# A hybrid S5 and gated-DeltaNet layer on one core: when the adaLN gate, shift and scale vectors are computed, and which queue loads their weights

## The chip, the cores and the metric

The kernel runs on one core of a Trainium2 chip. The metric is the device time of one execution in microseconds; lower is better. Engines are named as the profile names them: PE (matmul) with its weight loads PEld, DVE (vector), ACT (scalar), POOL (GpSimd) and SP (which here only issues DMAs). The program gives each engine one fixed order of instructions.

## The reference, cut to what matters

One layer, 512 tokens, width 2048, float32. `mod` gives six vectors of 2048: shift, scale and gate of the mixer, shift, scale and gate of the feed-forward part.

```
mod = (silu(c) @ w_ada + b_ada)                  # w_ada is 2048 x 12288: 100 MB
sh_m, sc_m, g_m, sh_f, sc_f, g_f = split(mod, 6)
h = layer_norm(x) * (1 + sc_m) + sh_m
p = h @ w_in
ys = s5(p) @ w_up_ssm;  yg = gated_deltanet(p) @ w_up_gdn        # "the mixers"
m = sigmoid(gate_ssm) * ys + sigmoid(gate_gdn) * yg              # "merge"
x = layer_norm(alpha * x + g_m * (m @ w_out), ln1_g, ln1_b)      # "output projection"
h = layer_norm(x) * (1 + sc_f) + sh_f
x = layer_norm(alpha * x + g_f * swiglu(h), ln2_g, ln2_b)        # feed-forward, hidden 5632
```

So g_m is first needed behind the output projection, sh_f and sc_f when the second norm is applied, and g_f when the first feed-forward sums are added.

## The kernel before

**Products.** Every large product is made of three float32r matmuls: weights and activations are each split into a high part (rounded on ACT: `whi`, `at`/`bt`) and a low part (the difference, on DVE: `wlo`). `Weights` walks one list of weight chunks of 512 KB: a load on SP into one of NB = 3 `raw` buffers, a cast to `whi` on ACT, a subtraction to `wlo` on DVE, then the matmuls into `pm` or `px_fo`. A `raw` buffer is free for the next load when its `wlo` has been computed.

**Stages, in order of PE's program.** Start (x, adaLN shift and scale of the mixer). The mixers: `gemm1` products of the eight DeltaNet heads, with the S5 scan and the DeltaNet chunk solve between them. At `switch()` the mixers' buffers are given up and two pools `bp` and `q2` (`P2`) take their place; then the remaining gate products, the GLU, and the merge. The output projection (`w_mix`, 64 chunks, 12 matmuls of 512 columns each) runs in two halves of 256 tokens. Then the feed-forward part: its first eight hidden tiles are computed in two token halves with matmuls of 256 columns, because the second norm of the second token half (`ln_half(1)`) is still under way; everything later is done on 512 tokens. `ln_half(hf)` normalizes (DVE, ACT, POOL), applies the second norm into `ld`, transposes on PE into `px_tr`, applies scale and shift `mod_f` on ACT (`f`) and splits the result into `h2`.

**What sets the order.** The kernel is written by a small planner (`Order`): side work is a set of generators ("lines"); each yield gives the tile that the line waits for, or a pause in microseconds of the planner's own clock, and after each matmul of the main line `tick()` writes the steps that are due by that clock. The result is one fixed order for each engine.

**The adaLN vectors.** Each vector is made in four lines of 512 columns. `ada_line` loads 16 chunks of 256 KB (128 rows x 512 columns) into `w1` (called `w` in the profile; four buffers, for a while also two `gg` buffers) and adds `chunk * ccol` into `aacc`: in the kernel before, eleven of the sixteen on DVE, five on ACT with POOL adding them into `aacc2`, and one DVE addition at the end; the loads are issued on POOL. `ada_row_line` then adds the bias, sums over partitions on PE (`px_ada<-aacc,half`) and writes 512 values to DRAM (`drow[2]`, in the profile `dgm`, for g_m; `drow[5]`, `dgf`, for g_f), from which they are later read back as rows (`grow`). `ada_cols_line` sums on PE with `one` and writes a piece of `mod_f`. The line `ada_rest` makes g_m (four row lines), then shift and scale (eight column lines), then g_f (four row lines), and is started in `switch()`. Three flags tell others how far it is: `k.ada_m` (waited for at the output projection's `grow`), `k.ada_f` (waited for in `ln_half` ahead of the transposes), `k.ada_done` (waited for ahead of the first feed-forward sums).

Of the kernel before, what the change touches and what calls it, by code (L numbers as in the profile page):

```python
# [11 lines left out]
F32 = mybir.dt.float32  # L12
# [949 lines left out]
def kernel(ctx, tc, x, c, w_ada, b_ada, w_in, lam_re, lam_im, log_dt, b_re, b_im, c_re, c_im,  # L962
# [5 lines left out]
    k = Ctx()  # L968
    o = k.o = Order()
# [152 lines left out]

    def ada_line(p, col0):

        acc = p.tile([128, 512], F32, name="aacc", tag="aacc", bufs=1)
        acc2 = P2[1].tile([128, 512], F32, name="aacc2", tag="aacc2", bufs=1) if P2 else None
        raws = []
        depth = 6 if k.ada_deep else 4

        def load():  # L1130
            k0 = 128 * len(raws)
            n = k.ada_n = k.ada_n + 1
            if not k.ada_deep or n % 6 < 4:
                raw = p.tile([128, 512], F32, name="w1", tag="w1", bufs=4)
            else:
                raw = P2[1].tile([128, 512], F32, name="gg", tag="gg", bufs=2)
            pool.dma_start(out=raw, in_=w_ada[0, k0:k0 + 128, col0:col0 + 512])
            raws.append(raw)
        for kt in range(16):
            while len(raws) < min(16, kt + depth):  # L1140
                load()
            yield raws[kt]
            while not P2 and o.free["v"] > o.clock + 0.2:
                yield 0.7
# [15 lines left out]
    def ada_cols_line(p, j, q, dst, plus):  # L1160

        acc = yield from ada_line(p, 2048 * j + 512 * q)
        yield acc
        ps = k.psum("ada")
        for i in range(4):
            pe.matmul(ps[:, i:i + 1], lhsT=acc[:, 128 * i:128 * i + 128], rhs=one, start=True, stop=True)
        v.scalar_tensor_tensor(out=dst, in0=ps[:, 0:4], scalar=plus, in1=bcol[:, 16 * j + 4 * q:16 * j + 4 * q + 4], op0=A, op1=A)

    def ada_row_line(p, j, q):

        acc = yield from ada_line(p, 2048 * j + 512 * q)
        for i in range(4):
# [6 lines left out]
        act.copy(acc[0:1, :], ps[0:1, :])  # L1179
        yield  # L1180
        ld.dma_start(out=drow[j][0:1, 512 * q:512 * q + 512], in_=acc[0:1, :])
# [164 lines left out]
    P2 = []  # L1346
    k.ada_m = k.ada_f = k.ada_done = k.ada_deep = False
    k.ada_n = 0

    def ada_rest():  # L1350
        for q in range(4):
            yield from ada_row_line(adp, 2, q)
        k.ada_m = True
        for q in range(4):
# [3 lines left out]
        for q in range(4):  # L1358
            yield from ada_row_line(adp, 5, q)
        k.ada_done = True  # L1360


# [428 lines left out]
```

## Time and profile before

| | us |
|---|---|
| runs, median of 3 (lowest to highest) | 3185.92 (3182.63 to 3190.62) |
| profiled execution, its own time | 3192.52 |
| its span, first to last instruction | 3190.7 |
| PE busy in the span | 3039.6 (95%) |
| DVE, ACT, POOL busy | 1649.5, 976.4, 879.7 |
| mean granted TensorE clock | 0.976 |

Places in the span, read from the times of the matmuls: the mixers run to about 1082, when the first `w_ada` load of `ada_rest` is issued; remaining gates, GLU and merge to 1431; output projection 1431 to 1656; then the transposes of the first token half; the first feed-forward tiles on 256 tokens each from 1682 and 1790 to 1890; the rest on 512 tokens. A PE that is busy is not a PE at full rate: matmuls overlap, so the number of matmuls in a stretch says more than the busy time.

### The profile page before, as it was taken

How to read it: one execution, taken by the hardware profiler on the slowest of the kernel's cores; microseconds unless marked ns; L12 is line 12 of the kernel's file. 1: busy time of each engine (PE TensorE's matmuls, PEld its weight loads, DVE VectorE, ACT ScalarE, POOL GpSimd, SP SyncE). 2: the span in 40 equal slices, each digit the busy share in tenths (PEclk: the TensorE clock that was granted, in tenths of full speed). 3: DMA queues.
4: the chain of work that ended last, by engine and by line, in shares of the span. 5: the costliest groups of instructions: out<-in, count | busy, mean ns of one | idle time of the engine just before them, and what ended most of it. 6: DMA issues, size and time to landing. Idle time of an engine off the chain costs nothing.

```text
span 3190.7 us, 40575 instructions
## 1 busy us (share of the span) xinstructions
PE 3039.6 (95%) x15953; PEld 2507.5 (79%) x15953; DVE 1649.5 (52%) x2407; ACT 976.4 (31%) x1386; POOL 879.7 (28%) x997
## 2 busy tenths in 40 slices
PE   5899999999999999998878899999999999999997
PEld 3588788888788888886758798888888888888885
DVE  6536664566545377767778653333333333333338
ACT  3233333333333244334345531221222222222121
POOL 4824434434352143333344203002001100200202
PEclk8899999999999999999989999999999999999999
DMA  9644233333333488778878463333333333333333
GB/s 339 217 126 109 72 82 92 93 88 81 84 98 86 152 283 267 235 246 290 272 232 242 137 177 108 94 99 111 94 99 108 97 99 104 101 99 97 108 106 119
DMA packets 505344, 458.17 MB, mean 144 GB/s; under 512 B 56144, under 2 KB 403632, under 8 KB 505152
## 3 DMA queue, kind: packets, MB, share of 16 engines
q1 hardware_dynamic: 477472, 375.34, 39.1%
q0 software_dynamic: 20480, 67.13, 6.2%
q10 hardware_dynamic: 7200, 13.10, 1.1%
q8 instruction: 125, 2.05, 0.3%
q14 instruction: 67, 0.55, 0.1%
HBM read 435.60 MB, written 19.89 MB: 143 GB/s over the span
## 4 chain that ended last, share of the span: by engine, by line
PE 78%; DVE 7%; DMA 6%; POOL 3%; issue 3%; ACT 2%; SPq 1%; ACTq 0%; DVEq 0%; POOLq 0%
PE pm L211 56%; PE px_fo L211 14%; PE px_gd L211 3%; DMA raw<-in_w_mix_out_dram 3%; PE px_s L211 2%; DVE wlo L170 2%; DVE at L170 1%; SPq L170 1%; DVE aacc L170 1%; ACT whi L170 1%; DMA w<-in_w_ada_dram 1%; DMA raw<-in_ffn_w_in_dram 1%; PE px_u L211 1%; POOL eq L170 1%; PE px_ada L211 0%
## 5 line engine op out<-in xcount | busy, mean ns | idle before, releaser
L211 PE MATMUL pm<-at,whi 128*128 128x512 f32 (+1 forms) x3744 | 1142.6, 388 | 7.4 <-ACT whi L170 3.6
L170 DVE TENSOR_TENSOR wlo<-raw,whi 128x1024 fp32r<-128x1024 f32 x541 | 698.4, 1293 | 773.2 <-ACT whi L170 761.3
L170 ACT CAST whi<-raw 128x1024 fp32r<-128x1024 f32 x541 | 567.0, 1049 | 1068.0 <-PE pm L211 464.8
L211 PEld LDWEIGHTS pm<-at,whi 128*128 128x128 f32 x3744 | 681.5, 190 | 138.8 <-issue 4.1
L211 PE MATMUL pm<-at,wlo 128*128 128x512 f32 (+1 forms) x1872 | 715.4, 382 | 6.4 <-DVE wlo L170 6.4
L211 PE MATMUL pm<-bt,whi 128*128 128x512 f32 (+1 forms) x2464 | 682.1, 363 | 0.7 <-ACT whi L170 0.7
L211 PEld LDWEIGHTS pm<-bt,whi 128*128 128x128 f32 x2464 | 443.9, 190 | 72.4 <-ACT whi L170 1.1
L211 PE MATMUL pm<-bt,wlo 128*128 128x512 f32 (+1 forms) x1232 | 446.9, 363 | 5.7 <-DVE wlo L170 5.7
L170 POOL TENSOR_TENSOR at<-at,ld 128x512 f32<-128x512 f32 x80 | 120.5, 1537 | 1106.9 <-DVE ld L170 1106.9
L211 PEld LDWEIGHTS pm<-at,wlo 128*128 128x128 f32 x1872 | 355.6, 190 | 76.5 <-DVE wlo L170 8.0
L211 PE MATMUL px_fo<-whi,bt 128*128 128x512 f32 x960 | 298.8, 389 | 0.0
L211 PEld LDWEIGHTS pm<-bt,wlo 128*128 128x128 f32 x1232 | 233.6, 190 | 42.6 <-DVE wlo L170 6.9
L211 PEld LDWEIGHTS px_fo<-whi,bt 128*128 128x128 f32 x960 | 180.1, 188 | 37.4
L170 POOL DMA_DIRECT2D w<-in_w_ada_dram x237 | 128.7, 544 | 291.2 <-DVE aacc L170 178.6
L211 PE MATMUL px_fo<-wlo,bt 128*128 128x512 f32 x480 | 186.7, 389 | 0.0
L170 DVE SCALAR_TENSOR_TENSOR aacc<-w,ccol,aacc 128x512 f32<-128x512 f32 x148 | 135.6, 916 | 13.4 <-DMA w<-in_w_ada_dram 11.8
L211 PE MATMUL pm<-whi,bt 128*128 128x512 f32 x336 | 112.2, 404 | 13.1 <-DVE at L170 13.0
L170 POOL TENSOR_TENSOR aacc<-aacc,w 128x512 f32<-128x512 f32 x59 | 88.2, 1495 | 77.9 <-ACT w L170 77.4
L211 PE MATMUL px_fo<-whi,at 128*128 128x512 f32 x336 | 107.5, 389 | 1.7 <-ACT whi L170 1.7
L211 PEld LDWEIGHTS px_fo<-wlo,bt 128*128 128x128 f32 x480 | 90.1, 188 | 18.7
L170 DVE SCALAR_TENSOR_TENSOR gs<-gg,pm 128x512 f32<-128x512 f32 x36 | 24.8, 688 | 142.1 <-ACT gg L170 142.1
L211 PEld LDWEIGHTS pm<-whi,bt 128*128 128x128 f32 x336 | 65.5, 195 | 30.5 <-DVE at L170 16.0
(389 smaller groups left out, 3173.6 us busy)
## 6 DMA issues: line engine op xcount, KB each, us to landing
raw<-in_ffn_w_in_dram SPq DMA_DIRECT2D x208, 512.0 KB, 4.0
raw<-in_w_in_dram SPq DMA_DIRECT2D x146, 512.0 KB, 3.7
w<-in_w_ada_dram POOLq DMA_DIRECT2D x237, 256.0 KB, 4.6
raw<-in_ffn_w_out_dram SPq DMA_DIRECT2D x88, 512.0 KB, 3.7
wad<-in_w_ada_dram SPq DMA_DIRECT2D x64, 512.0 KB, 5.8
raw<-in_w_mix_out_dram SPq DMA_DIRECT2D x64, 512.0 KB, 5.8
raw<-in_w_up_gdn_dram SPq DMA_DIRECT2D x16, 512.0 KB, 4.0
raw<-in_w_up_ssm_dram SPq DMA_DIRECT2D x16, 512.0 KB
```

What stands on the lines that cost most here:

```text
L170: r = f(*a, **kw)
L211: r = self.e.matmul(out, **kw)
```

## The change

`ada_rest` is taken apart. A new line `ada_gate` makes g_m beside the mixers; it is started as soon as its pool exists, before the first S5 and DeltaNet work. `ada_rest` still starts in `switch()`, waits for `k.ada_m`, makes shift and scale as before, and then g_f. The row lines (g_m and g_f) are now paced: a pause of 6.0 (g_m) or 3.5 (g_f) planner microseconds at each chunk, loads three chunks ahead instead of four or six, the loads issued on SP instead of POOL, and all sixteen chunks on DVE with no share for ACT and POOL. Beside the mixers a paced step also waits until the planner sees DVE free. `ada_row_line` waits for `acc` ahead of its write to DRAM.

```diff
-    def ada_line(p, col0):
+    def ada_line(p, col0, pace):
         acc = p.tile([128, 512], F32, name="aacc", tag="aacc", bufs=1)
-        acc2 = P2[1].tile(...) if P2 else None
-        depth = 6 if k.ada_deep else 4
+        acc2 = None if pace else P2[1].tile(...)
+        deep = k.ada_deep and not pace
+        depth = 3 if pace else 6 if deep else 4
+        eng = k.sync if pace else pool
...
-            pool.dma_start(out=raw, in_=w_ada[0, k0:k0 + 128, col0:col0 + 512])
+            eng.dma_start(out=raw, in_=w_ada[0, k0:k0 + 128, col0:col0 + 512])
...
             yield raws[kt]
-            while not P2 and o.free["v"] > o.clock + 0.2:
+            if pace:
+                yield pace
+            while pace and not P2 and o.free["v"] > o.clock + 0.2:
                 yield 0.7
...
-    def ada_row_line(p, j, q):
+    def ada_row_line(p, j, q, pace):
...
         act.copy(acc[0:1, :], ps[0:1, :])
-        yield
+        yield acc
         ld.dma_start(out=drow[j][0:1, 512 * q:512 * q + 512], in_=acc[0:1, :])
...
+    def ada_gate():
+        for q in range(4):
+            yield from ada_row_line(adp, 2, q, 6.0)
+        k.ada_m = True
     def ada_rest():
-        for q in range(4):
-            yield from ada_row_line(adp, 2, q)
-        k.ada_m = True
+        while not k.ada_m:
+            yield 2.0
...
-            yield from ada_row_line(adp, 5, q)
+            yield from ada_row_line(adp, 5, q, 3.5)
         k.ada_done = True
+
+    o.add(ada_gate())
```

**SP at the start of the output projection.** `raw<-in_w_mix_out_dram` is a weight chunk of 512 KB, `w_...<-in_w_ada_dram` a chunk of 256 KB for g_f, `grow` the row of g_m, `at<-in_x_dram` the residual. Before:

```order
L170 DMA gs<-dg_115 128x512
L170 DMA raw<-in_w_mix_out_dram 128x2x512 x2
L170 DMA grow<-dgm 128x512
L170 DMA at<-in_x_dram 128x512
L170 DMA raw<-in_w_mix_out_dram 128x2x512
L170 DMA at<-in_x_dram 128x512
L170 DMA raw<-in_w_mix_out_dram 128x2x512 x8
```

And changed:

```order
L170 DMA gs<-dg_115 128x512
L170 DMA raw<-in_w_mix_out_dram 128x2x512
L170 DMA w_12174<-in_w_ada_dram 128x512
L170 DMA raw<-in_w_mix_out_dram 128x2x512
L170 DMA w_12210<-in_w_ada_dram 128x512
L170 DMA w_12250<-in_w_ada_dram 128x512
L170 DMA grow<-dgm 128x512
L170 DMA at<-in_x_dram 128x512
L170 DMA raw<-in_w_mix_out_dram 128x2x512
```

The gate's chunks now stand between the weight chunks in SP's own queue: 39 of them between the first and the last of the 64 `w_mix` chunks, and 22 behind the last; 64 others stand in the mixers. On POOL, 128 loads (shift and scale) are left of 256.

**PE at the end of the output projection.** `pm<-whi,at` and `pm<-whi,bt` are its matmuls, `pm<-bt,whi 128x256` the first of the feed-forward part, `px_tr` the transposes of the first token half (32 in all, four of 128x128 for each of eight groups). Before:

```order
L211 MATMUL pm<-wlo,bt 128x512
L211 MATMUL pm<-whi,bt 128x512
L216 MATMUL px_tr<-cst,ld 128x128 x12
L211 MATMUL px_ada<-aacc,half 128x512
L216 MATMUL px_tr<-cst,ld 128x128 x16
L211 MATMUL pm<-bt,whi 128x256 x2
L211 MATMUL pm<-bt,wlo 128x256
```

And changed, the last two groups of transposes:

```order
L216 MATMUL px_tr<-cst,ld 128x128 x4
L211 MATMUL pm<-whi,at 128x512
L211 MATMUL pm<-wlo,at 128x512
L211 MATMUL pm<-whi,at 128x512 x2
L211 MATMUL pm<-wlo,at 128x512
L211 MATMUL pm<-whi,at 128x512
L216 MATMUL px_tr<-cst,ld 128x128 x4
L211 MATMUL pm<-whi,at 128x512
L211 MATMUL pm<-wlo,at 128x512
L211 MATMUL pm<-whi,at 128x512
L211 MATMUL pm<-whi,bt 128x512
```

Before, 28 of the 32 transposes stand behind the last matmul of the output projection; now the first group stands 114 matmuls ahead of that end and the last 15 ahead of it, and nothing stands between the projection and the feed-forward part.

**DVE in the mixers**, at the first head's solve: `g_X`, `g_T`, `g_TT` are its steps, `wlo` a weight chunk's low part. Before:

```order
L170 TENSOR_TENSOR g_X<-px_gd,cmix 128x256
L170 TENSOR_TENSOR gt<-g_G,gcol 128x4
L170 TENSOR_TENSOR wlo<-raw,whi 128x1024
L170 TENSOR_TENSOR g_T<-g_T,px_gd 128x256
L170 TENSOR_TENSOR g_TT<-g_TT,px_gd 128x256
L170 TENSOR_TENSOR g_X<-px_gd,cmix 128x256
```

And changed:

```order
L170 TENSOR_TENSOR g_X<-px_gd,cmix 128x256
L170 TENSOR_TENSOR gt<-g_G,gcol 128x4
L170 TENSOR_TENSOR wlo<-raw,whi 128x1024
L170 SCALAR_TENSOR_TENSOR aacc<-w_2171,ccol,aacc 128x512
L170 TENSOR_TENSOR g_T<-g_T,px_gd 128x256
L170 TENSOR_TENSOR g_TT<-g_TT,px_gd 128x256
```

A chunk's multiply-add now stands between the solve's steps, ahead of what PE waits for next.

More of the change, by code (lines that the diff above doesn't have):

```diff
@@ L1121, in rstd_of @@
         pool.tensor_tensor(out=tmp, in0=tmp, in1=mhalf, op=ALU.pow)
-    def ada_line(p, col0):
+    def ada_line(p, col0, pace):
         acc = p.tile([128, 512], F32, name="aacc", tag="aacc", bufs=1)
-        acc2 = P2[1].tile([128, 512], F32, name="aacc2", tag="aacc2", bufs=1) if P2 else None
+        acc2 = None if pace else P2[1].tile([128, 512], F32, name="aacc2", tag="aacc2", bufs=1)
         raws = []
-        depth = 6 if k.ada_deep else 4
+        deep = k.ada_deep and not pace
+        depth = 3 if pace else 6 if deep else 4
+        eng = k.sync if pace else pool
         def load():
@@ L1132, in load @@
             n = k.ada_n = k.ada_n + 1
-            if not k.ada_deep or n % 6 < 4:
+            if not deep or n % 6 < 4:
                 raw = p.tile([128, 512], F32, name="w1", tag="w1", bufs=4)
@@ L1160, in ada_cols_line @@
     def ada_cols_line(p, j, q, dst, plus):
-        acc = yield from ada_line(p, 2048 * j + 512 * q)
+        acc = yield from ada_line(p, 2048 * j + 512 * q, 0)
         yield acc
@@ L1167, in ada_cols_line @@
         v.scalar_tensor_tensor(out=dst, in0=ps[:, 0:4], scalar=plus, in1=bcol[:, 16 * j + 4 * q:16 * j + 4 * q + 4], op0=A, op1=A)
-    def ada_row_line(p, j, q):
-        acc = yield from ada_line(p, 2048 * j + 512 * q)
+    def ada_row_line(p, j, q, pace):
+        acc = yield from ada_line(p, 2048 * j + 512 * q, pace)
         for i in range(4):
```

## The prediction

> **What bounds the kernel now.** I began with the slices of the page: PE's busy share, the clock it was granted, the DMA share.
>
> ```profile
> PE   5899999999999999998878899999999999999997
> PEclk8899999999999999999989999999999999999999
> DMA  9644233333333488778878463333333333333333
> ```
>
> Each digit is a fortieth of the span, 80 us. PE is at nine tenths nearly everywhere, but not from the nineteenth slice to the twenty-third, where DMA is high and the clock dips. So I cut the span at its stages: mixers, gates to merge, output projection, gap, first and second feed-forward half, steady stretch.
>
> ```profile
> core 0: us, PE busy (x) PEld busy (x) DVE busy (x) ACT busy (x) POOL busy (x), PEclk, DMA share, GB/s
> 150.00:1082.00 932.00, 912.49 (x6071) 759.77 (x6070) 518.78 (x1105) 302.31 (x548) 356.54 (x390) 0.99 0.34 93
> 1082.00:1431.00 349.00, 349.00 (x1551) 287.89 (x1550) 243.11 (x283) 134.11 (x170) 131.18 (x183) 1.00 0.78 255
> 1431.00:1656.00 225.00, 198.37 (x808) 154.82 (x807) 174.38 (x210) 88.70 (x100) 81.81 (x104) 0.94 0.84 273
> 1656.00:1682.00 26.00, 9.29 (x33) 5.75 (x32) 14.98 (x29) 16.24 (x32) 17.05 (x20) 0.58 0.57 179
> 1682.00:1790.00 108.00, 96.87 (x751) 93.24 (x750) 90.30 (x118) 51.08 (x73) 44.78 (x46) 0.97 0.74 218
> 1790.00:1890.00 100.00, 91.06 (x726) 89.95 (x727) 50.93 (x65) 50.77 (x77) 8.82 (x6) 0.95 0.54 153
> 2000.00:2200.00 200.00, 200.00 (x884) 165.62 (x883) 64.57 (x65) 46.72 (x53) 6.02 (x4) 1.00 0.33 99
> ```
>
> ```profile
> L211 PE MATMUL px_ada<-one,aacc x32: 169/250/353, 1435.2 to 1569.8; 128*128 128x1 f32 x32
> 1808.89 91.17 PE pm L211 x754
> ```
>
> The last row is PE undisturbed: 200 us / 884 = 0.226 us for a matmul of 512 columns. The gates-to-merge row runs at that rate (349 / 1551 = 0.225): nothing is lost there. The projection needs 768 x 0.226 = 174 us, and some 7 us for the 40 short ones beside them (the first of the two rows: 0.25 each, partly overlapped), 181; it takes 225. So 44 us are lost. The gap is 26 us with only 33 PE instructions; a feed-forward half needs 768 x 0.120 = 92 us (matmuls of 256 columns; 91.17 / 754 in the second row, a piece of the chain), takes 108 and 100. Together some 44 + 21 + 12 + 4 = 81 us can be had, and nearly all of it lies between 1431 and 1890, where `ada_rest` is running beside other work. What ends the waits in the projection:
>
> ```profile
> ACT whi L170 <- DMA raw<-in_w_mix_out_dram: 90.9, 34, 5.8
> DVE wlo L170 <- ACT whi L170: 46.3, 27, 4.8
> PE pm L211 <- DVE at L170: 13.0, 7, 5.0
> PE pm L211 <- DVE wlo L170: 7.5, 11, 1.4
> ```
>
> ACT waits for weight chunks in flight, DVE for ACT, PE for DVE. It is the DMA: SP itself waits only for buffers that DVE has yet to free, and once issued, a chunk takes long to land.
>
> ```profile
> SPq L170 <- DVE wlo L170: 134.2, 55, 7.6
> DMA packets 30806, 61.41 MB, mean 273 GB/s; under 512 B 2718, under 2 KB 6597, under 8 KB 30793
> raw<-in_w_mix_out_dram SPq DMA_DIRECT2D x59, 512.0 KB, 5.8
> w<-in_w_ada_dram POOLq DMA_DIRECT2D x74, 256.0 KB, 5.6
> raw<-in_ffn_w_in_dram SPq DMA_DIRECT2D x208, 512.0 KB, 4.0
> ```
>
> The same 512 KB land in 4.0 us (median) in the feed-forward part, 5.8 here, beside 74 adaLN chunks.
>
> **Part by part.** All against the profiled execution, 3192.5 us (1.8 outside its span of 3190.7), which is 6.6 above the median 3185.9; I subtract the change from the median at the end.
>
> *Projection.* Of its 61.4 MB, 74 x 0.262 = 19.4 MB are adaLN chunks. In the new order about 40 are left there (39 between its first and last weight chunk): 34 x 0.262 = 8.9 MB less, so 52.5 MB. At the same 273 GB/s that is 192 us, 33 less than now. Bounds: 181 (PE's own need, 44 less) and 225 (nothing, if the three raw buffers and DVE set the pace). I take 33: the DMA share of 0.84 and 90.9 us of ACT waiting for chunks put this stage nearest to the bytes. DVE does not take the gain back:
>
> ```profile
> L170 DVE TENSOR_TENSOR wlo<-raw,whi 128x1024 fp32r<-128x1024 f32 x64 | 84.6, 1331 | 46.3 <-ACT whi L170 46.3
> L170 DVE SCALAR_TENSOR_TENSOR aacc<-w,ccol,aacc 128x512 f32<-128x512 f32 x47 | 40.4, 861 | 0.8 <-DMA w<-in_w_ada_dram 0.5
> L170 ACT CAST whi<-raw x541: 1027/1051/1084, 44.0 to 3123.7; 128x1024 fp32r<-128x1024 f32 x181
> ```
>
> 47 multiply-adds now; with all sixteen of a line on DVE, 40 chunks are some 40 of them (35 us), no additions of two halves, so about 5 us less in a stretch 30 us shorter. What ACT (its whole share of five in sixteen) and POOL lose there costs nothing and brings nothing: neither is waited for in the rows above.
>
> The Trainium skill ("DMA: Bandwidth & Descriptors", "Issuing engines are not separate DMA queues") holds that DMAs started on sync, scalar or gpsimd end on the same 16 engines and that another issuer saves only issue time. By that rule the move to SP buys no bandwidth and my term is the bytes alone, as worked out above; the sum stays 3138, where a queue of its own that mattered would lead to the second rival's 3111. The trace agrees with the page in so far as both kinds of chunk land slowly together (5.8 and 5.6 us).
>
> *Gap.* PE stands there because `ld`, the normalized tile, is late, group after group:
>
> ```profile
> PE px_tr L216 <- ACT ld L170: 12.8, 6, 6.9
> 1656.13 0.60 PE L216 MATMUL px_tr<-cst,ld 128*128 128x128 f32 x4
> 1663.62 0.48 PE L216 MATMUL px_tr<-cst,ld 128*128 128x128 f32 x1 [6.89 <-ACT ld L170]
> ```
>
> The new order has the first transposes 114 matmuls (26 us) ahead of the projection's end and the last 15 ahead. Their 32 transposes then cost about 5 us on PE inside the projection, so 21 of the 26 can go. How late `ld` will be by the clock I can't see; between 0 and 21 I take 15, because the lead of 26 us is as long as the whole gap, while DVE, ACT and POOL still do the same work.
>
> *First feed-forward half.* Waits of PE there:
>
> ```profile
> PE pm L211 <- DVE wlo L170: 9.6, 10, 2.2
> L170 POOL DMA_DIRECT2D w<-in_w_ada_dram x24: 536/538/588, 1685.8 to 1756.7; - x24
> ```
>
> 24 adaLN chunks stand there now, 22 in the new order behind the last `w_mix`, but all on DVE: 22 multiply-adds instead of 17. The transposes of the second token half stand from 108 matmuls ahead of the half's end instead of 48, so that less of them is waited for. I take -4, between +5 (DVE) and -12. *Second half*: -2, between 0 and -4; g_f's last line ends with the first half in PE's order, 768 matmuls (92 us) ahead of its first use, so `k.ada_done` is not waited for.
>
> *Mixers.* Added: 64 loads on SP, 64 multiply-adds on DVE, and for each line four bias additions, a matmul and a copy that only moved. Prices:
>
> ```profile
> L170 DVE SCALAR_TENSOR_TENSOR aacc<-w,ccol,aacc x148: 734/747/2083, 1106.6 to 1765.9; 128x512 f32<-128x512 f32 x148
> L170 DVE SCALAR_TENSOR_TENSOR aacc<-cst,bacol,aacc x32: 342/346/352, 1129.5 to 1771.6; 128x128 f32<-128x128 f32 x32
> PE px_s L216 <- DMA s5C<-in_ssm_c_im_dram: 8.5, 6, 2.7
> PE px_gd L211 <- ACT g_th L170: 4.9, 2, 4.4
> PE px_gd L216 <- DVE g_th L170: 3.5, 2, 1.8
> ```
>
> DVE gets 64 x 0.747 + 16 x 0.346 = 53 us, on 518.8 of 932. It has room (0.56 to 0.61), but a multiply-add stands in front of whatever comes next: at worst all 48 us reach PE, at best none. PE waits only 19.5 us in 932 now (932 - 912.5), of which little is DVE's (3.5 in two waits). If all its waits grew with DVE's load, by a tenth, that were 2 us, and with the slower clock behind a wait twice that: +4. DMA there is at 0.34 and gets 16.8 MB over 932 us, 18 GB/s on 93: nothing. SP issues 64 more in 932 us; a load waits for the buffer of four chunks earlier, whose multiply-add the pause puts at least 12 planner microseconds back, so it holds up no weight chunk behind it. Cover gone, that is one chunk of 256 KB in front of a weight chunk, under 1 us at 273 GB/s.
>
> *Gates to merge.* Eight column lines stand where four row lines and three to four column lines stood; they start a little later and end some 31 us ahead of the projection. DMA is at 0.78 with PE losing nothing; I take +2, between 0 and +8 (denser column lines, whose loads still come from POOL).
>
> Sum: -33 - 15 - 4 - 2 + 4 + 2 = -48. From the median: 3186 - 48 = **3138 us**.
>
> **Rivals.**
>
> *The projection keeps its pace* (chance 0.18): three raw buffers and the round through landing, ACT and DVE set it, not the bytes. For: SP waits 134.2 us for `wlo`; loads for g_f now wait behind such a chunk in SP's queue, as they did not in POOL's. Against: with 4.0 us landing the round is 4.0 + 1.05 + 1.33 = 6.4 for three chunks, 2.1 each, below PE's 2.7 (12 x 0.226). Without the projection's 33: -15, 3171.
>
> *PE becomes the bound of the projection* (0.13): one queue instead of two, chunks landing in 4.0 again, and the gap closes wholly: -44 - 21 - 10 - 4 + 4 = -75, 3111. The Trainium skill (same page, "Queues, rings and completion order") says that each DMA engine takes turns between queues packet by packet; by that rule a weight chunk in SP's queue paid for every chunk in POOL's, and would now pay only for those ahead of it. The row for it is 5.8 against 4.0; that the turns are the cause no run here shows yet.
>
> *Slower by the mixers* (0.07): DVE's multiply-adds stand in the chain of the DeltaNet solve, where PE takes its 64x64 products from DVE's `g_X` and `g_T` at once. If each of the 64 put PE off by its 0.75 us and as much again at a slow clock, 96 us are added: 3186 - 54 + 96 = 3228. It decides from 54 / 64 = 0.84 us lost for each. Against: the pause looks for a free DVE, and only 3.5 us of waits are DVE's now.
>
> *No change* (0.08): what the projection gains, the feed-forward halves give back: the 22 chunks of g_f with all work on DVE, in the halves where PE waits 9.6 us for `wlo`, and a gap that stays since DVE, ACT and POOL are as late as before. -33 + 20 + 4 + 2 = -7, 3179.
>
> **How the numbers follow.** My own case has 0.54 and holds 3120 to 3158. A measurement of this kernel can tell 0.3%, 9.6 us, from no change (the three runs span 8 us). Faster by more: 0.54 + 0.18 + 0.13 = 0.85; same 0.08; slower 0.07. The range from 3108 to 3176 takes in the second and the third case and leaves out the last two and 0.04 below.
>
> **What would show it.** Right: the projection in 185 to 200 us with a landing under 5.3 us and ACT's wait for `in_w_mix_out` halved; `px_tr` inside it, the gap under 12 us; PE losing under 10 us more in the mixers, which still take 932 to 940. Wrong: `aacc` as releaser of `px_gd` or `pm` in the mixers; DVE waiting for `w`, loaded late behind a blocked chunk on SP; the first half above 108 us.

## The result and the profile after

The changed kernel takes 3158.4 us (median of 4 runs, 3158.2 to 3160.0) where the kernel before, run beside it, takes 3188.3 (4 runs, 3182.6 to 3190.7): a ratio of 0.991, 95% interval 0.9893 to 0.9927. It is faster by some 30 us, and 20 us slower than the 3138 of the prediction. The profiled execution took 3158.2 us, its span is 3156.5.

The slices of the page, to be laid beside those of before:

```profile
PE   5899999999999999999999999999999999999997
PEclk9899999999999999999999999999999999999998
DMA  9654234334333368777777653333333333333333
```

PE's dip from the nineteenth slice to the twenty-third is gone, and the DMA share is 7 from the nineteenth slice to the twenty-second, where three of the four had 8; in the mixers, from the third slice on, it has risen by a tenth in places. The stages of the changed kernel, cut where its own matmuls begin them: mixers, gates to merge, projection, first and second feed-forward half.

```profile
150.00:1115.00 965.00, 923.78 (x6087) 763.97 (x6086) 590.71 (x1178) 303.13 (x550) 371.14 (x390) 0.98 0.38 106
1115.00:1462.00 347.00, 347.00 (x1562) 287.82 (x1561) 236.97 (x274) 129.17 (x162) 115.50 (x159) 1.00 0.76 251
1462.00:1666.00 204.00, 191.03 (x808) 151.87 (x807) 158.95 (x202) 90.42 (x111) 29.05 (x18) 0.97 0.79 254
1666.00:1775.00 109.00, 101.23 (x807) 98.29 (x806) 88.81 (x134) 57.14 (x85) 26.79 (x18) 0.98 0.74 215
1775.00:1954.00 179.00, 178.76 (x1150) 163.65 (x1149) 80.24 (x92) 58.44 (x73) 20.23 (x15) 1.00 0.50 149
```

The same cut of the first half in the kernel before, by its 768 matmuls of 256 columns:

```profile
1682.00:1808.50 126.50, 106.43 (x805) 101.69 (x805) 97.29 (x131) 66.09 (x102) 52.63 (x52) 0.95 0.66 195
```

To compare kernels whose stages lie at other times, the table below and the experiments cut by matmuls counted in the trace, which are the same in all: the mixers are the stretch from the 300th to the 2950th large matmul (those into `pm`), the projection runs from the first to the last matmul of `w_mix`, the gap to the first matmul of 256 columns, and the first half over 768 of those. The row of the second half takes in its own 768 (93.2 us before, 92.9 after) and the 384 matmuls of 512 columns behind them, the first feed-forward sums (`px_fo`).

| us | before | after | difference | predicted |
|---|---|---|---|---|
| start, to the 300th large matmul | 229.4 | 226.9 | -2.5 | |
| mixers | 883.9 | 916.4 | +32.5 | +4 |
| gates to merge | 317.8 | 319.0 | +1.2 | +2 |
| output projection | 224.8 | 203.3 | -21.5 | -33 |
| gap | 25.9 | 0.2 | -25.7 | -15 |
| first feed-forward half | 126.7 | 108.8 | -17.9 | -4 |
| second half, with the first sums | 180.1 | 179.8 | -0.3 | -2 |
| the rest | 1202.1 | 1202.1 | 0.0 | |
| span | 3190.7 | 3156.5 | -34.2 | -48 |

Behind the mixers 65 us were gained in three places, where 52 were forecast; half of them went back in the mixers.

**The projection.** The waits there, as engine, tile, what it waited for, us in total, times, longest:

```profile
ACT whi L170 <- DMA raw<-in_w_mix_out_dram: 64.6, 30, 7.8
DVE wlo L170 <- ACT whi L170: 40.5, 27, 6.9
PE pm L211 <- DVE wlo L170: 4.8, 5, 2.0
PE pm L211 <- DVE at L170: 3.2, 3, 1.9
PE px_tr L216 <- ACT ld L170: 3.1, 4, 1.9
```

and its DMA (the last number of an issue is the median landing in us):

```profile
DMA packets 30472, 51.83 MB, mean 254 GB/s; under 512 B 2153, under 2 KB 6249, under 8 KB 30461
raw<-in_w_mix_out_dram SPq DMA_DIRECT2D x59, 512.0 KB, 5.5
```

ACT's wait for weight chunks fell from 90.9 to 64.6 us, not to half. The landing went from 5.8 to 5.5, but that says little: the trace holds a landing for only 8 of the 64 chunks (10 before), from 3.7 to 8.8 us, and the median of all eight is 4.3. The bytes are near what the prediction said (51.8 MB for 52.5); they came at 254 GB/s, not at 273. `px_tr` now stands inside the projection and waits 3.1 us there: that is all that is left of the gap.

**The mixers.** First the stretch before, then after (us; PE busy; PEld, DVE, ACT and POOL busy; granted clock; DMA share; GB/s):

```profile
229.39:1113.28 883.89, 865.51 (x5850) 719.92 (x5848) 502.43 (x1086) 284.18 (x521) 339.17 (x349) 0.99 0.34 93
```

```profile
226.90:1143.27 916.37, 875.15 (x5856) 722.88 (x5854) 567.42 (x1154) 285.01 (x523) 345.19 (x339) 0.98 0.37 105
```

PE stands idle for 41.2 us (916.37 - 875.15) instead of 18.4, and the same matmuls take 9.6 us longer, at a granted clock of 0.98 instead of 0.99. By the trace's clock records PE had half its clock for 41 us of this stretch instead of 24, in pieces of 3.4 to 10.2 us, and each piece begins within 6 us of the start of a wait of PE of over a microsecond, though not every such wait has one behind it. So a wait can cost more than its own length. DVE works 65 us more, not the 53 that the prediction priced. What PE waits for:

```profile
PE px_s L216 <- DMA s5C<-in_ssm_c_im_dram: 10.0, 7, 2.7
PE px_gd L216 <- DVE g_th L170: 9.6, 3, 5.5
PE px_gd L211 <- DVE g_X L170: 7.4, 4, 2.9
PE px_gd L211 <- ACT g_th L170: 7.1, 3, 6.2
PE px_ada L211 <- DVE aacc L170: 4.2, 2, 2.4
```

The wait for `s5C`, a load on SP, was there before (8.5). What grew are the waits for `g_X` and `g_th`, tiles of the DeltaNet solve, which come late from DVE; hardly ever is `aacc` itself what PE waits for. One of these places in the timeline (start, us, engine, operation), DVE, then POOL, then PE:

```profile
650.80 2.25 DVE L170 SCALAR_TENSOR_TENSOR g_q<-g_th,g_q 128x512 f32<-128x512 f32 x1 [3.57 <-ACT g_th L170]
652.97 0.41 DVE L170 TENSOR_TENSOR g_X<-px_gd,cmix 128x256 f32<-128x256 f32 x1
653.31 2.52 DVE L170 SCALAR_TENSOR_TENSOR aacc<-w,ccol,aacc 128x512 f32<-128x512 f32 x1
```

```profile
648.52 2.02 POOL L170 TENSOR_TENSOR s_V<-PAr,s5bb 128x1024 f32<-128x1024 f32 x1
650.51 1.99 POOL L170 TENSOR_TENSOR s_W<-PAi,s5bb 128x1024 f32<-128x1024 f32 x1
652.58 2.69 POOL L170 TENSOR_TENSOR s_V<-s_V,s_W 128x1024 f32<-128x1024 f32 x1
```

```profile
653.44 0.62 PE L211 MATMUL px_gd<-g_X,g_TT 64*64 64x64 f32 x7 [2.92 <-DVE g_X L170]
```

`g_q<-g_th,g_q` and the multiply-add are both operations of 0.7 us; here they take 2.25 and 2.52. `g_q` ends half a microsecond behind POOL's `s_W`, the multiply-add half a microsecond behind POOL's second `s_V`, and that `s_V`, which runs across the end of `g_q`, takes 2.69 where its shortest in the stretch takes 2.37. `g_X` stands behind `g_q`, and PE waits 2.92 us for `g_X`. Over the whole stretch (ns, min/median/max):

```profile
L170 DVE SCALAR_TENSOR_TENSOR aacc<-w,ccol,aacc x57: 736/744/2536, 272.1 to 1142.3; 128x512 f32<-128x512 f32 x57
```

```profile
L170 DVE SCALAR_TENSOR_TENSOR g_q<-pm,cw,g_q x24: 739/748/750, 238.6 to 962.8; 128x511 f32<-128x511 f32 x8, 128x510 f32<-128x510 f32 x8, 128x509 f32<-128x509 f32 x8
L170 DVE SCALAR_TENSOR_TENSOR g_q<-g_th,g_q x8: 678/1564/2875, 287.4 to 973.9; 128x512 f32<-128x512 f32 x8
```

Four of the eight `g_q<-g_th,g_q` take over 2.2 us; in the kernel before two of the eight did. Of the 57 multiply-adds, 30 run while POOL has no operation under way, and none of them takes over 0.747 us; of the other 27, 17 take over 0.76, up to 2.54, and 15 of these 17 end 0.55 us after an operation of POOL that ran beside them. The same form of operation with one input in PSUM (`pm`) never varies, 739 to 750 ns, though 18 of the 24 run beside an operation of POOL. So a DVE operation that reads two tiles of SBUF and one of POOL's keep each other waiting. The Trainium skill ("SBUF — State Buffer", "Who interferes with whom") states this: a DVE instruction with two SBUF inputs contends with a GpSimd instruction that reads SBUF, and the later one blocks until the earlier is done. By that rule a 0.75 us operation that comes second lasts until POOL's is done; the timeline agrees, and shows half a microsecond more.

### The profile page after: what moved, and what is told of

Read it like the earlier page. It is cut to its first block, busy times and chain, and to the rows that moved or that the text cites. A ratio compares the mean times of both kernels' runs of the same rounds, so it can differ in the third digit from the quotient of the medians.

```text
span 3156.5 us, 40449 instructions
## 1 busy us (share of the span) xinstructions
PE 3025.4 (96%) x15953; PEld 2496.2 (79%) x15953; DVE 1676.8 (53%) x2439; ACT 950.7 (30%) x1346; POOL 779.5 (25%) x837
## 4 chain that ended last, share of the span: by engine, by line
PE 76%; DVE 7%; DMA 5%; issue 4%; POOL 4%; ACT 2%; SPq 1%; ACTq 0%; DVEq 0%; POOLq 0%
PE pm L211 55%; PE px_fo L211 14%; PE px_gd L211 3%; PE px_s L211 2%; DMA raw<-in_w_mix_out_dram 2%; DVE wlo L170 2%; DVE at L170 1%; SPq L170 1%; ACT whi L170 1%; DVE aacc L170 1%; DMA raw<-in_ffn_w_in_dram 1%; PE px_u L211 1%; POOL eq L170 1%; DMA at<-in_x_dram 1%; PE px_ada L211 1%
## 5 line engine op out<-in xcount | busy, mean ns | idle before, releaser
L170 DVE TENSOR_TENSOR wlo<-raw,whi 128x1024 fp32r<-128x1024 f32 x541 | 686.2, 1270 | 777.7 <-ACT whi L170 760.4
L211 PEld LDWEIGHTS px_fo<-whi,bt 128*128 128x128 f32 x960 | 180.1, 188 | 37.4
L170 DVE SCALAR_TENSOR_TENSOR aacc<-w,ccol,aacc 128x512 f32<-128x512 f32 x186 | 169.5, 911 | 6.7 <-DMA w<-in_w_ada_dram 5.7
L170 POOL DMA_DIRECT2D w<-in_w_ada_dram x107 | 57.7, 541 | 146.0 <-DVE aacc L170 112.7
L170 POOL TENSOR_TENSOR rs<-rs,mhalf 128x1 f32<-128x1 f32 (+1 forms) x13 | 10.9, 839 | 321.7 <-DVE rs L170 317.5
L170 DVE TENSOR_TENSOR gs<-gs,pm 128x512 f32<-128x512 f32 x36 | 24.7, 687 | 119.9 <-PE pm L211 119.9
```

The source lines that it names most:

```text
L170: r = f(*a, **kw)
L211: r = self.e.matmul(out, **kw)
```

## The experiments

The theory after the first look: the multiply-adds on DVE cost the mixers their 32 us, not by their own 0.75 us but where they meet POOL. Its rivals: the loads of g_m in SP's queue hold up other loads; or the planner's new order of everything else is worse by chance. Behind the mixers: which part of the change closed the gap, and what still bounds the projection. All that was measured on the mixers stands here, with the ratio to the kernel before on the same chip; PE idle is the length of the stretch less PE's busy time, "g_q, g_z, g_v" is the sum of the 24 DeltaNet operations of the form shown above.

| kernel | median us | ratio (95%) | mixers | PE idle there | multiply-adds there: count, us | g_q, g_z, g_v, us |
|---|---|---|---|---|---|---|
| before | | | 883.9 | 18.4 | 2, 2.5 | 20.8 |
| after | 3158.4 | 0.9910 (0.9893–0.9927) | 916.4 | 41.2 | 57, 57.1 | 27.9 |
| m1_no_madd | 3148.1 | 0.9876 (0.9858–0.9895) | 890.5 | 21.4 | none | 20.9 |
| m10_no_madd_pace_5 | 3148.2 | 0.9868 (0.9852–0.9885) | 891.9 | 21.7 | 2, 1.5 | 21.5 |
| m7_pace_5 | 3188.1 | 0.9997 (0.9988–1.0006) | 930.9 | 43.8 | 59, 62.2 | 29.5 |
| m6_madd_twice | 3188.5 | 0.9995 (0.9984–1.0006) | 918.6 | 41.8 | 112, 124.4 | 19.6 |
| m11_both_free | 3199.1 | 1.0028 (1.0015–1.0041) | 928.3 | 46.3 | 58, 49.3 | 33.6 |
| m9_gm_on_act_pool | 3172.1 | 0.9943 (0.9926–0.9959) | 918.2 | 39.5 | 6, 5.5 | 27.9 |
| m2_gm_on_pool_queue | 3148.0 | 0.9878 (0.9863–0.9892) | 905.2 | 32.3 | 57, 62.9 | 18.5 |
| m5_when_pool_free | 3196.1 | 1.0028 (1.0014–1.0041) | 890.7 | 20.8 | 39, 34.7 | 19.1 |
| m3_gm_after_mixers | 3168.8 | 0.9944 (0.9928–0.9960) | 882.8 | 17.8 | 2, as before | 20.3 |
| m12_free_then_fast | 3153.8 | 0.9883 (0.9863–0.9902) | 894.7 | 22.1 | 43, 39.6 | 20.2 |

How well the stretch repeats is seen where it has the same order: the changed kernel and two experiments that differ from it only behind the mixers (m4, m8) have 916.4, 919.8 and 920.2 there.

**m1_no_madd: the lines without their multiply-adds.** Loads, bias additions, matmuls and copies stay.

```diff
             while pace and not P2 and o.free["v"] > o.clock + 0.2:
                 yield 0.7
+            if pace == 6.0 and kt:
+                continue
```

> The changed kernel without 60 of the 64 multiply-adds of g_m beside the mixers (only the first chunk of each line is used, so g_m is made of a sixteenth of its weights); all loads, the bias additions, the sums on PE and the writes stay. In the changed kernel the output projection begins at 1462, in the kernel before at 1431. DVE theory (the multiply-adds stand between the steps of the DeltaNet solve, and PE waits): it begins at 1425 to 1437 again and the time is 3127 +- 8. Queue theory (the loads on SP hold up the weight chunks and the mixers' own loads): still at 1462, 3158. Order theory (the planner writes another order of the same work, and any other order gives or takes tens of us): anywhere between 1425 and 1465.

```profile
228.28:1118.77 890.49, 869.05 (x5856) 721.15 (x5855) 505.67 (x1098) 286.04 (x523) 333.15 (x340) 0.98 0.38 108
```

The mixers fall to 890.5: without the multiply-adds, and in the order that the planner then writes, 26 of the 32.5 us are gone; 7 are left for the loads and the rest. That is 0.43 us for each of the 60 left out, between nothing and the 0.84 of the third rival. The kernel as a whole gains 10 us only, since in this order the projection takes 210.8 and the first half 113.0.

**m2_gm_on_pool_queue: the loads of g_m on POOL's queue again.**

```diff
-        eng = k.sync if pace else pool
+        eng = k.sync if pace == 3.5 else pool
```

> The changed kernel with the 64 loads for g_m beside the mixers issued on POOL instead of SP; the multiply-adds stay on DVE. Queue theory: the output projection begins at 1431 again, 3127. DVE theory: at 1455 to 1465 as now, 3158 +- 6 (POOL's issue of 0.54 us each adds 35 us to an engine that is busy 0.38 of the time).

The mixers take 905.2, 11 less, and the whole kernel some 10 less. Read alone this spoke for the queue. But PE's idle time fell where `g_q` and its like fell too (27.9 to 18.5 us), not where a load was late: the wait for `s5C`, which SP loads, even grew from 10.0 to 22.0 us. Queue and places changed together here; the next two runs show what places alone can do, so the 11 us can't be credited to the queue.

**m7_pace_5: another pause, the same work.**

```diff
-            yield from ada_row_line(adp, 2, q, 6.0)
+            yield from ada_row_line(adp, 2, q, 5.0)
```

> The pause between the chunks of g_m is 5.0 planner microseconds instead of 6.0; the same loads, the same multiply-adds, only other places in the mixers (the last line ends some 190 matmuls earlier). DVE theory and queue theory: the same work at other places, mixers 916 within 5, median 3158 within 5. Order theory: another draw, mixers 905 to 926, median 3147 to 3169; a difference of that size here says that differences of 10 us between the kernels of this study need no other cause.

```profile
227.70:1158.58 930.88, 887.13 (x5858) 732.57 (x5856) 581.54 (x1163) 286.53 (x526) 351.89 (x349) 0.96 0.37 105
```

```profile
PE px_gd L211 <- DVE g_X L170: 18.0, 9, 5.3
PE px_s L216 <- DMA s5C<-in_ssm_c_im_dram: 14.1, 6, 4.2
PE px_gd L216 <- DVE g_th L170: 4.6, 2, 3.8
```

All three expectations were too narrow: a ratio of 0.9997 instead of 0.9910, all of the gain lost by a sixth off a pause. 14.5 us are in the mixers. The wait for `g_X` went from 7.4 to 18.0, but other waits fell, and PE's idle time in all rose only from 41.2 to 43.8: 12 of the 14.5 us are the same matmuls at a lower granted clock (busy 887.1 instead of 875.2, clock 0.96 instead of 0.98; half the clock for 68 us instead of 41, in nine pieces instead of seven). The clock alone can differ by some of that in one order: m8, with the mixers of the changed kernel, had it halved for 51 us. Another 8.6 come behind them (gates to merge 327.6), where g_m ends earlier and PE waits 6.6 us in one piece for the `aacc` of a line. The worst place in the mixers, on DVE:

```profile
327.58 2.60 DVE L170 SCALAR_TENSOR_TENSOR aacc<-w,ccol,aacc 128x512 f32<-128x512 f32 x1
330.11 2.50 DVE L170 SCALAR_TENSOR_TENSOR g_q<-g_th,g_q 128x512 f32<-128x512 f32 x1
332.53 0.41 DVE L170 TENSOR_TENSOR g_X<-px_gd,cmix 128x256 f32<-128x256 f32 x1
```

A multiply-add and the `g_q` behind it run beside POOL's `s_V` and `s_W`, 5.1 us together instead of 1.4.

**m10_no_madd_pace_5: that other pause without the multiply-adds.** The edit is that of m1 on top of that of m7.

> Pause of 5.0 planner microseconds as in m7_pace_5 (mixers 930.9 there), but fifteen of a line's sixteen multiply-adds of g_m are left out (g_m is made of a sixteenth of its weights); loads, bias additions, matmuls and copies of the lines stay. Overlap theory (PE loses where a multiply-add meets a tensor operation of POOL, both run two to three times as long, and PE's next DeltaNet product stands behind it on DVE; where that happens is a matter of the place): without multiply-adds the place cannot matter, mixers 885 to 897 as at pause 6.0 (890.5), median 3145 to 3155. Order theory (the places of all other instructions, which a new pause also shifts, make the difference): mixers stay 905 to 935, median 3165 to 3190.

```profile
224.44:1116.38 891.94, 870.25 (x5858) 720.70 (x5856) 511.68 (x1105) 286.82 (x525) 340.03 (x349) 0.98 0.38 109
```

891.9, as with the pause of 6.0 (890.5). Without the multiply-adds the mixers of the two orders differ by 1.4 us; with them by 14.5. So most of the loss in these two kernels comes with the multiply-adds, and its size is a matter of their places. That any new order of the rest costs or gains tens of us in the mixers, as the order theory had it, is not seen in these two. POOL's own operations are stretched less than the expectation put it (2.37 to 2.69 us in the timeline above). (Behind them the wait at `px_ada` stays: gates to merge 332.1.)

**m6_madd_twice: each multiply-add of g_m made twice.**

```diff
                 v.scalar_tensor_tensor(out=acc, in0=raws[kt], scalar=sc, in1=acc, op0=M, op1=A)
+                if pace == 6.0:
+                    junk = p.tile([128, 512], F32, name="ajunk", tag="ajunk", bufs=1)
+                    v.scalar_tensor_tensor(out=junk, in0=raws[kt], scalar=sc, in1=acc, op0=M, op1=A)
```

> Each of the 64 multiply-adds of g_m in the mixers is made twice (the second into a tile that nobody reads); loads and everything else as in the changed kernel. DVE theory (PE loses what stands behind a multiply-add, some 26 of the 32 us): 64 more of 0.75 to 2.7 us put another 20 to 32 us on the mixers, 936 to 948 instead of 916, median 3176 to 3190. Queue theory (the loads in SP's queue hold up others): mixers 916 within 5, median 3158 within 5. Order theory (the planner's different order alone makes the difference): any of -10 to +10, not more.

```profile
222.35:1140.93 918.58, 876.76 (x5855) 723.01 (x5854) 629.39 (x1210) 286.85 (x524) 348.92 (x338) 0.98 0.37 105
```

DVE has 62 us more to do and PE loses 2. A fixed price per multiply-add, on which my expectation rested, is refuted. The planner knows of the second one and puts the chunks elsewhere; at these places the DeltaNet's own operations stay short (19.6 us). The kernel is 30 us slower all the same: projection 215.5, gap 2.9, first half 122.1, in an order in which g_m ends 45 matmuls later.

**m11_both_free: wait until the planner sees POOL free too.** With a short pause, so that all 64 still fit, and g_m's loads on POOL's queue.

```diff
-        eng = k.sync if pace else pool
+        eng = k.sync if pace == 3.5 else pool
...
-            while pace and not P2 and o.free["v"] > o.clock + 0.2:
+            while pace and not P2 and max(o.free["v"], o.free["p"]) > o.clock + 0.2:
...
-            yield from ada_row_line(adp, 2, q, 6.0)
+            yield from ada_row_line(adp, 2, q, 1.0)
```

> A multiply-add of g_m or g_f waits until by the planner's clock both DVE and POOL are free (before: DVE alone); the pause of g_m is 1.0 so that all four lines still end within the mixers; the loads of g_m go out on POOL's queue. Overlap theory: all 64 multiply-adds in the mixers, but few beside POOL's operations: sum of them near 60 x 0.747 = 45 us, mixers 888 to 902, median 3130 to 3150. Count theory (each multiply-add on DVE costs PE its 0.4 us wherever it stands): mixers 910 to 920, median 3152 to 3165. Order theory: anything from 890 to 930.

The multiply-adds did get short: 49.3 us for 58. The mixers took 928.3 nevertheless, so the overlap theory, that the mixers lose only where a multiply-add meets POOL, is refuted as it stood. The whole is 41 us slower than the changed kernel: 12 in the mixers, 10 more to the merge, where PE waits for the `aacc` of a line again, and 16 in the projection. What grew instead is `g_q`, `g_z` and `g_v`, to 33.6 us. The longest of them, on DVE and on POOL:

```profile
436.59 3.93 DVE L170 SCALAR_TENSOR_TENSOR g_q<-g_th,g_q 128x512 f32<-128x512 f32 x1 [2.87 <-ACT g_th L170]
440.44 0.41 DVE L170 TENSOR_TENSOR g_X<-px_gd,cmix 128x256 f32<-128x256 f32 x1
```

```profile
435.97 2.03 POOL L170 TENSOR_TENSOR s_V<-PAr,s5bb 128x1024 f32<-128x1024 f32 x1
437.95 2.01 POOL L170 TENSOR_TENSOR s_W<-PAi,s5bb 128x1024 f32<-128x1024 f32 x1
```

No multiply-add stands near: a DeltaNet operation of 0.7 us waited out two of POOL's. What moved the DeltaNet's steps against the S5 steps on POOL was not separated: the multiply-adds' new places, or the 64 load issues that POOL has here besides (three of them, 1.7 us, stand right ahead of this `s_V`).

**m9_gm_on_act_pool: the work on ACT and POOL.** ACT multiplies, POOL adds, DVE does neither.

```diff
-            while pace and not P2 and o.free["v"] > o.clock + 0.2:
+            while pace and not P2 and o.free["p"] > o.clock + 0.2:
...
+            elif pace == 6.0:
+                act.activation(raws[kt] if kt else acc, raws[kt], AF.Copy, scale=sc)
+                if kt:
+                    pool.tensor_tensor(out=acc, in0=acc, in1=raws[kt], op=A)
```

> g_m in the mixers without DVE: ACT multiplies each chunk by its scalar, POOL adds the 128x512 product to the sum, and the pause waits for a free POOL; loads on SP's queue, pause 6.0, g_f as in the changed kernel. If DVE's multiply-adds are the loss (without them 890.5 and 891.9 in two orders, with them 916 to 931 in three): mixers 886 to 898, median 3130 to 3145, unless ACT's or POOL's part does the same harm. If it is any work on a third engine that shifts the DeltaNet's own long DVE operations beside POOL's (g_q, g_z, g_v over their shortest: 11.6 us in the changed kernel, 4.5 without multiply-adds): POOL is busier by 60 adds, so more of such meetings, mixers 905 to 930, median 3148 to 3175, and g_q, g_z and g_v again over 10 us above their shortest.

```profile
L170 POOL TENSOR_TENSOR aacc<-aacc,w 128x512 f32<-128x512 f32 x60 | 88.1, 1468 | 162.4 <-ACT w L170 161.5 <-ACT gt L170 0.7
```

918.2, as in the changed kernel with none of its 60 multiply-adds on DVE, and `g_q`, `g_z`, `g_v` are at 27.9 us again. This is what the second expectation had forecast, and it fits a meeting of the two engines, from whichever side the work is added; that POOL is 92 us busier here (437.6 instead of 345.2) may cost something by itself too, which was not tried. POOL's addition takes 1468 ns in the mean, DVE's whole multiply-add 744 in the median.

**m5_when_pool_free: the wait for POOL at the old pause.** Of the edit of m11 the `while` line alone.

> The changed kernel, but beside the mixers a multiply-add waits until the planner sees both DVE and POOL free. In the changed kernel a multiply-add takes 0.75 us when POOL is idle and up to 2.5 us beside a POOL addition (mean 1.01). Contention theory (these long ones are what PE waits for): the mean falls below 0.85 and the projection begins at 1440 to 1450, 3135 to 3148. DVE theory without contention (0.75 us in the wrong place is enough): 1455 to 1465, 3152 to 3162.

```profile
PE px_ada L211 <- DVE aacc L170: 27.8, 2, 21.1
```

At the pause of 6.0 the condition is seldom met: only 39 multiply-adds stand in the mixers, which take 890.7. But g_m, and so everything behind it, ends late: the line above is from the end of the projection and the feed-forward halves, where PE stands at the sums of g_f's lines (second half 213.6 us), and the kernel is slower than before.

**m3_gm_after_mixers: g_m stays behind the mixers, g_f is paced as in the change.** g_m is made as before, in `ada_rest`, shared with ACT and POOL.

```diff
     def ada_rest():
-        while not k.ada_m:
-            yield 2.0
+        for q in range(4):
+            yield from ada_row_line(adp, 2, q, 0)
+        k.ada_m = True
...
-    o.add(ada_gate())
```

> The changed kernel with g_m made in switch() again, ahead of shift and scale, unpaced and on POOL's queue as in the kernel before; only g_f is paced and on SP. The mixers carry nothing: the output projection begins at 1431 +- 6 by the DVE and by the queue theory. If the gain behind it comes from fewer adaLN bytes there, the projection takes 215 to 225 as before (the column lines stand in it again) and the whole 3175 to 3190; if it comes from pacing and from SP's queue, the projection takes about 203 as in the changed kernel and the whole about 3127.

```profile
1423.00:1651.30 228.30, 201.78 (x834) 157.68 (x833) 176.43 (x220) 99.39 (x125) 71.23 (x76) 0.95 0.77 257
1761.60:1958.50 196.90, 185.23 (x1159) 168.12 (x1158) 101.06 (x126) 59.21 (x74) 21.75 (x16) 0.96 0.55 165
```

```profile
PE px_ada L211 <- DVE aacc L170: 11.7, 1, 11.7
```

This divides the result. The gap is 0.2 and the first half 110.3 here too: both were won by the new treatment of g_f (paced, loaded by SP, all on DVE), not by moving g_m; m4 below keeps the gap closed, and most of the first half's gain, without the loads on SP. Moving g_m is the step from this kernel to the changed one: projection 228.3 to 203.3, second half 196.9 to 179.8, mixers 882.8 to 916.4. So 42 us are won and 34 lost, and 5 more ahead of the mixers (221.9 to 226.9); in the medians the move is worth 10 us of the 30.

**m8_no_gf: g_f from the first chunk of each line alone.**

```diff
-            while len(raws) < min(16, kt + depth):
+            if pace == 3.5 and kt:
+                continue
+            while len(raws) < min(1 if pace == 3.5 else 16, kt + depth):
```

> g_f is made of the first chunk of each line alone, a sixteenth of its weights: 60 loads of 256 KB and 60 multiply-adds less beside projection and first half. Bytes theory (DMA sets the pace of the projection): about 36 of its chunks gone, 49.8 - 9.4 = 40.4 MB, at 254 GB/s 159 us, so PE's own need of 181 to 186 sets it; first half 95 to 100 instead of 109; median 3125 to 3135. Pace theory (my first rival: three raw buffers, DVE and ACT set it): projection 198 to 203, first half 104 to 109, median 3150 to 3158.

```profile
1468.10:1658.80 190.70, 183.06 (x807) 147.62 (x806) 131.31 (x167) 91.09 (x112) 27.99 (x18) 1.00 0.68 218
```

Median 3143.1, ratio 0.9859 (0.9844 to 0.9873), between the two theories: the projection falls by 12.6 us to 190.7 with 10 MB less (218 GB/s x 190.7 us = 41.6 MB instead of 51.8), and the first half to 103.2. At 254 GB/s these 41.6 MB need 164 us, less than PE's own 181 to 186, so by the bytes alone PE would have set the stage; 5 to 10 us more remain with nearly all of g_f's chunks gone. The 12.6 us are not the bytes' alone either, for the multiply-adds went with them (DVE busy for 131.3 us instead of 159.0). So something besides bytes holds the projection; how much each has in the changed kernel is not separated.

**m4_gf_on_pool_queue: the loads of g_f on POOL's queue, those of g_m on SP's.**

```diff
-        eng = k.sync if pace else pool
+        eng = k.sync if pace == 6.0 else pool
```

> The loads of g_f go out on POOL's queue again, those of g_m stay on SP's. If a queue of their own lets the adaLN chunks take turns with the weight chunks (my second rival, and the rule of the Trainium skill, DMA: Bandwidth & Descriptors, on turns between queues): projection 210 to 220 instead of 203, landing of in_w_mix_out 5 us and more instead of 4.3. If only the bytes count: 203 within 3, median 3158 within 5. If in SP's queue the chunks of g_f stand ahead of weight chunks (as g_m's seemed to in the mixers, where POOL's queue gave 11 us): projection 195 to 200, halves 2 to 4 shorter, median 3148 to 3154.

```profile
raw<-in_w_mix_out_dram SPq DMA_DIRECT2D x59, 512.0 KB, 4.5
w<-in_w_ada_dram POOLq DMA_DIRECT2D x39, 256.0 KB, 4.8
```

Median 3163.8, ratio 0.9919 (0.9902 to 0.9935), which overlaps that of the changed kernel. The projection takes 200.1 instead of 203.3, the first half 113.1 instead of 108.8; the landing row has 4.5 us beside POOL's queue and 5.5 in SP's own, again from the few chunks whose landing the trace holds (9 of 64 here, 4.0 over all of them, against 4.3). A queue of their own makes no difference to the weight chunks that these rows can show. The rule of turns between queues, on which my second rival stood, shows no effect on the stage's time here; the other rule of the Trainium skill ("DMA: Bandwidth & Descriptors", "Issuing engines are not separate DMA queues"), that another issuer saves only issue time, agrees with these rows.

**m12_free_then_fast: m5's places in the mixers, and no lateness behind them.**

```diff
             if pace:
-                yield pace
+                yield pace if pace < 4.0 or not P2 else 0.5
-            while pace and not P2 and o.free["v"] > o.clock + 0.2:
+            while pace and not P2 and max(o.free["v"], o.free["p"]) > o.clock + 0.2:
...
-            yield from ada_row_line(adp, 5, q, 3.5)
+            yield from ada_row_line(adp, 5, q, 2.5)
```

> In the mixers as in m5_when_pool_free (a multiply-add waits until by the planner's clock DVE and POOL are both free; pause 6.0): some 39 of the 64 stand there, at the places where they cost 7 us. Behind the mixers' end the pause of g_m falls to 0.5 and that of g_f is 2.5 instead of 3.5, so that g_f's last line ends 120 matmuls ahead of the first half's end, not 770 behind it. Place theory (what a multiply-add costs PE is a matter of where it stands beside POOL's operations): mixers 888 to 894, gates to merge 317 to 322 with some 24 multiply-adds more and nothing lost, projection 203 to 212, gap under 3, halves 108 to 114 and 180: the sum 3130 to 3150, the fastest here. Count theory, or lateness: what the mixers gain comes back as a wait in projection or halves (projection 215 to 228, second half 190 to 214 as in m3 and m5), 3155 to 3175.

```profile
226.13:1120.84 894.71, 872.64 (x5853) 723.32 (x5852) 542.09 (x1135) 284.60 (x521) 338.29 (x337) 0.98 0.36 103
```

894.7 in the mixers, 319.1 to the merge with nothing lost, projection 211.7, gap 1.8, first half 116.8, second 179.2. 22 us are kept in the mixers and 18 given back in projection, gap and first half: 3153.8 us, ratio 0.9883, between the two expectations. This and m2 (0.9878) are the fastest kernels here that compute the whole layer. The interval of m2 (0.9863 to 0.9892) lies just below that of the changed kernel (0.9893 to 0.9927), that of m12 overlaps it.

## Why the prediction came out right, and where its terms were off

The sign, the range and the place of the gain were right; the sum was 20 us too low on the median. Some 14 of the 20 are its terms, which erred in both directions: it had mixers and projection 40 us too short, gap and first half 25 too long. That these errors offset each other is luck: the first two alone would have made 3178 of the 3138, outside the range. The other 6 are that the profiled execution before lay 6.6 us above its median, and that of the changed kernel on it.

*Mixers (+4, measured +32.5).* This is the term that failed. Its steps "53 us on DVE" and "DVE has room" priced a multiply-add alone, at 0.747 us, and took PE's waits to grow by a tenth; they more than doubled (18.4 to 41.2 us), and the clock behind them took another 9.6. The row that I quoted for the price already held the warning, 734/747/2083 ns: a maximum of 2.1 us that I did not follow up. m1 and m10 show that 26 and 39 us go when the multiply-adds go, at the two pauses; m9 and m11 that it does not need the multiply-adds themselves to be slow. The sign to look for was also wrong: `aacc` as releaser of `px_gd` never appears; the lateness passes through `g_X` and `g_th`, whose DVE operations are the program's own. "Slower by the mixers" had the right place; its 0.84 us per multiply-add was not reached (0.43 in the changed kernel, 0.65 in m7: 39.0 us over 60), but m7, a sixth off one pause, came to no gain at all. Of the signs of being right, the mixers' (under 10 us more of waits), the projection's (185 to 200) and ACT's wait (halved) did not appear; the gap's did. Of the signs of being wrong, the first half came out at 108.8, just above its mark of 108, though 18 us were won there by the same cut, and DVE's wait for `w` did not grow.

*Projection (-33, measured -21.5).* The bytes were right and the rate was not: 254 GB/s, not 273. m8 shows that bytes alone do not set the stage. The first rival's round through three buffers holds part of the time, as its row (SP waiting for `wlo`, ACT for chunks) said. What SP waits for there, in the changed kernel:

```profile
SPq L170 <- DVE wlo L170: 91.8, 54, 4.8
SPq L170 <- DVE aacc L170: 19.0, 19, 5.0
```

The second row was 3.1 us before: a load for g_f that waits for its buffer now holds up the weight chunks behind it in SP's queue. It is worth little, for in m4, where those loads are in POOL's queue, the stage is only 3 us shorter. Neither the round nor the bytes alone give 203. The row of 5.8 us against 4.0, on which both the bytes and the second rival leaned, rests on the landings of 10 of 64 and 25 of 208 chunks.

*Gap (-15, measured -25.7).* The lead of 26 us in the order was enough; the transposes wait 3.1 us inside the projection. m3 shows that this came with g_f's treatment alone.

*First half (-4, measured -17.9).* The mechanism was right (transposes ahead, PE's wait for `wlo` from 9.6 to 1.7 us in the halves); the size was off because I cut the half at 1790. Its 768 matmuls of 256 columns end at 1808.5: it took 126.7 us, and 35 could be had over the floor of 92. The cut at 1790 gave 16 and 8 for the two halves, of which the prediction booked 12 and 4.

*Second half (-2, measured -0.3) and gates to merge (+2, measured +1.2)* were right, though in the second half nothing could be had: its 768 matmuls took 93.2 us before.

*The Trainium skill's rule on issuing engines* was weighed rightly: 3111 by a queue of its own did not come, and m4 found no worth in the queue.

What stays open: which meetings on DVE and POOL decide the mixers' time in a given order. The stretched time of the multiply-adds and of `g_q`, `g_z`, `g_v` goes with the loss in most rows of the table, but they do not add up to it: m2 has its multiply-adds stretched by more than the changed kernel (62.9 - 57 x 0.747 = 20.3 us, against 14.5) and loses less, m6 by far more (40.7) and loses the same. The waits of PE bring some order into it. Without those for `s5C` (10.9 us in the changed kernel, 22.3 in m2, 18.2 in m6), PE's idle time in the mixers is 28 to 33 us in the four kernels whose `g_q`, `g_z`, `g_v` take 27.9 us or more (after, m7, m9, m11), and 9 to 15 in all others of the table, m2 among them, but for m6 with 24. So the stretched operations of the solve go with the waits on DVE, and what m2 still loses is a wait for `s5C`; why that comes later there was not tried. Why the projection takes between 200 and 219 us in nine kernels that load 37 to 40 adaLN chunks there was not tried either. Whether m2's 11 us in the mixers are the queue or the places is open too; m7 shows that places alone make more.

## What to carry to other kernels

Before work is added to DVE, look at the maximum and not only the median of its like in the trace, and at what POOL runs at that moment: here a multiply-add of 0.75 us on DVE lasted up to 2.5 us beside one of POOL's, and what stood behind it on DVE was what PE waited for. A kernel whose order is fixed by a planner should be measured at two or three neighbouring settings of the number that is changed before the change is judged: here a pause of 5 instead of 6 undid all of the gain. And a stage's floor is found by counting its matmuls to the last, not by cutting it at a round time.

## What the runs showed of the hardware

A DVE multiply-add of 128x512 floats takes 0.736 to 0.747 us while POOL is idle, and up to 2.54 us beside POOL's operations on 128x1024 floats (2.0 us); up to 3.93 us was seen for a DeltaNet operation of 0.68 (m11). POOL pays too: 2.69 instead of 2.37 us in the timeline above. The form with one input in PSUM stays at 739 to 750 ns beside POOL. In the mixers the granted clock was halved for 24 us before and 41 after, each time within 6 us of the start of a wait of PE of over a microsecond. With the same order of instructions the mixers took 916.4, 919.8 and 920.2 us in three executions, so differences of 10 us and more between kernels are more than their noise.
